# Pinned expert weights, GpSimd stores of the normed rows, and a smaller DMA scratch

## The chip, the cores and the metric

One core of a Trainium2 chip runs the whole program in one launch. The metric is device time in microseconds (us), the median of several runs. One run was also profiled; all rows below are from that execution.

## The reference, cut to what matters

Two layers (DEPTH = 2) of a model of width 1024 over 512 latent tokens and, in the first layer, 256 context tokens. In each layer an attention mix (neighbourhood attention, a gated recurrence, differential attention) is projected by `w_out` and added to `x`; then every token goes to two of 32 experts.

```python
for l in range(2):
    ...                                                    # mix: y_na, y_rg, y_diff
    xl = xl + ga1 * (concat([y_na, y_rg, y_diff]) @ w_out[l])
    hl2 = rmsnorm(xl, g_ffn[l]) * (1 + sc2) + sh2          # "normed rows"
    # two-level router: 1 group of 4, then 2 of its 8 experts
    expert_id, weight = route(hl2)
    # each expert: (silu(x @ w1) * (x @ w3)) @ w2, D = 1024, F = 512
    xl = xl + ga2 * moe(hl2, expert_id, weight)            # layer 0: also the context rows
return rmsnorm(xl, g_final)
```

The kernel loads the weights of all 32 experts in each layer, 32 x 6 tiles of 1 MB: 384 tiles, 402.7 MB of the 544.74 MB that the profile shows read from HBM.

## The kernel before, in words

The kernel is written against a tile framework: code asks for tiles from pools, and a scheduler puts the instructions of each engine in a fixed order. A new tile of a full pool waits until the last reader of the tile that it replaces is done. Every engine runs its own instructions, and its own DMA issues, strictly in order.

Weights. A tile "w" is 128 x 2048 f32, 1 MB. An expert takes six: w1, w3, w2 in two halves each (`eparts`, L1015). The tiles come round robin from the list `wcycle` (L1008): pools `wta` (NWA tiles), `wt2` (NW2 - NWA), `wt` (6, shared with other loads of the stages before) and `wt3` (4); W0 says where in the list the six of `wt` stand. The ring has 6 + 6 + 4 = 16 tiles in layer 0 and 8 + 6 + 4 = 18 in layer 1. All loads go through SyncE's queue (SP), except the first SPIN of a layer, which ScalarE (ACT) issues (L1024).

Pinned experts. The last three experts, 29 to 31 (NPIN = 3), run first, whatever the router says, so that their 18 tiles can be loaded before it has spoken ("pins"). The generator `ping` issues one pin at each call: NWA of them inside the attention stage (L1149), some in the loop over token tiles until PINT are out (L1391), then all but HELD (L1410), and the last HELD only behind `idn` (L1503), the last vector of the routing (L1505). The other 29 experts are sorted by their number of tokens on the chip; their loads need the expert's number (`sid`, L1818).

Loop over token tiles (L1378 on; six in layer 0, four in layer 1). `wmm` is TensorE's projection (L1101); `upd` (L1345) adds it to X on VectorE (L1347), squares it on ACT (L1348) and makes the factor r on GpSimd (L1350, L1351). `normed` (L1354) makes hp = X * r * a2 on VectorE (L1357), adds s2 on VectorE for tiles 1 and 3 (HVV) and on GpSimd for the others (L1358), and stores hp to the DRAM tensor h2d (L1359). `turn_x` transposes X (L1367) and `logits` (L1374) gives the router's values, which L1396 scales by r.

Routing (L1325 to L1503) is a chain of small VectorE instructions with a few matmuls; it ends in idx_t, sid and idn. `weights` (L1780 to L1806) makes the experts' weights for the output, not for the order.

Experts. For each one GpSimd gathers its rows from h2d (`xg`, L1826), TensorE transposes them (L1628), multiplies by w1 and w3 (L1638 for 32 rows, L1642 and L1643 for 64, L1648 for 128), ACT copies the product (`hs`, L1658), TensorE transposes again (L1667, L1672) and multiplies by w2 (L1695, L1700, L1701, L1706); VectorE scales the result (L1562, L1564) and GpSimd scatters it to the DRAM tensor yd (L1517). In layer 0 alone each expert also has its scale made ahead by ACT in a tile "yl" (L1553); there are three such tiles, and one is free again when its scatter has landed.

Of the kernel before, what the change touches and what calls it, by code (L numbers as in the profile page):

```python
# [56 lines left out]
RGR = (1.0, 0.85)  # L57
FLG = (1, 1)
WST = (0, 0)
HELD = (4, 3)  # L60
DMO = ("gsXw", "gsXw")
FLL = (3, 1)
LTS = ("aaatmghsscccbbbbcccccMccocHccc", "")
# [24 lines left out]
UE = ("SV", "SV")  # L88
OSV = ((0, 1), (0, 1))
OHV = ((0, 1, 2, 3, 4, 5), (0, 1, 2, 3, 4, 5))  # L90
SPIN = (2, 0)
PINT = (6, 8)
FEX = (0, 0)
DOR = ("asctwfv", "asctwfv")
CHD = ("TV", "TV")
# [7 lines left out]
AHEAD = 1  # L103
CXN = ((2, 0, 0), (0, 0, 2))
XNB = (6, 2)
NW2 = (6, 8)
NWA = (0, 2)
NWS = (9, 9)
W0 = (4, 12)
LAM = (1, 1)  # L110
DIAG = (1, 1)
SCT = (1, 1)
# [138 lines left out]
def program(tc, a, out, dbg=None):  # L251
    nc = tc.nc
# [22 lines left out]
    V, S, G, T = [Chained(e_) for e_ in (nc.vector, nc.scalar, nc.gpsimd, nc.tensor)]  # L275
    Y = nc.sync
# [9 lines left out]
    h2d = [dr.tile([NT, D], F32, name=f"h2d{l}") for l in range(2)]  # L286
# [165 lines left out]
    for l in range(2):  # L452
# [551 lines left out]
        sid = xp_.tile([1, 33], I32, name="sid")  # L1004
        nw2 = NW2[l] - NWA[l]
        wta = P.open(f"wta{l}")
        wcount, held = [0], [None]
        wcycle = [(lambda: wta, NWA[l])] * NWA[l] + [(lambda: wt2, nw2)] * nw2 + [(lambda: wt3, 4)] * 4  # L1008
        wcycle[W0[l]:W0[l]] = [(wt, 6)] * 6

# [4 lines left out]
        def eparts(e, eng=Y, tail=False):  # L1015
            for nm in ("w1", "w3", "w2"):
# [3 lines left out]
                for h in range(2):  # L1020
                    pl, nb = wcycle[wcount[0] % len(wcycle)]
                    w = wtile(pl() if callable(pl) else pl, nb)
                    wcount[0] += 1
                    held[0] = (Y if wcount[0] > SPIN[l] else eng).dma_start(w.rearrange("p (k f) -> p k f", k=2 * n if cut else n),  # L1024
                                                               src[:, :, 512 * h:512 * h + 512] if cut else src[:, n * h:n * h + n, :])
# [91 lines left out]
        def wparts():  # L1117
            todo = [(hf, t, k0) for hf in range(2) for t in range(nt) for k0 in KO]
            ahead = [ysplit(*z_[1:]) for z_ in todo[:YA[l]]]
            for n_, (hf, t, k0) in enumerate(todo):  # L1120
# [28 lines left out]
                if n_ == NWS[l]:  # L1149
                    for _ in range(NWA[l]):  # L1150
                        next(ping)
# [202 lines left out]
        def normed(t, hp, r1):  # L1354
            a2, s2 = vs[t // 4]
            hv = hp.rearrange("t (k p) -> t p k", p=128)
            V.scalar_tensor_tensor(hv, kp(X[:, t, :]), r1, kp(a2), op0=ALU.mult, op1=ALU.mult)  # L1357
            (V if t in HVV[l] else G).tensor_tensor(hv, hv, kp(s2), op=ALU.add)  # L1358
            Y.dma_start(h2d[l][128 * t:128 * t + 128, :], hp)  # L1359

        def turn_x(t):
            xT2 = op.tile([128, 8, 128], F32, name="xT2", bufs=1)
# [15 lines left out]
        for t in range(nt + 1):  # L1378
            if t < nt:
                k67 = (7,) if t in p6 else (6, 7)  # L1380
                p_ = p6[t] if t in p6 else pss()
                wmm(p_[:, 0:512], t, 0, k67)
            if t > 0:
                xT2 = turn_x(t - 1)
            if t < nt:
                wmm(p_[:, 512:1024], t, 1, k67)
            if t > 0:
                pg = logits(t - 1, xT2)
            if t < nt:
                hps[t] = upd(t, p_)  # L1390
                for _ in range(8 // nt + 1):  # L1391
                    if wcount[0] < PINT[l]:
                        next(ping)
            if t > 0:
                hp, r1 = hps.pop(t - 1)
                V.scalar_tensor_tensor(lg[:, t - 1, :], pg[:, 0:36], r1, crow[(t - 1) // 4], op0=ALU.mult, op1=ALU.add)  # L1396
                normed(t - 1, hp, r1)
            if t == nt - 2:
                top2(0, nt - 2)
# [9 lines left out]

        for _ in range(6 * NPIN - wcount[0] - HELD[l]):  # L1410
            next(ping)
# [710 lines left out]
        for k_ in SEQ[l]:  # L2122
# [4 lines left out]
            else:  # L2127
                combine(*k_)
                if k_[1]:
                    n_, t = k_[0], order[k_[0]]  # L2130
# [32 lines left out]
```

## Time and profile before

| | |
|---|---|
| median of 3 runs | 2043.89 us (2037.6 to 2045.23) |
| profiled execution | 2047.19 us, its span 2045.6 us |
| TensorE busy | 1692.9 us, 83% of the span |
| VectorE, ScalarE, GpSimd busy | 901.0, 575.3, 407.1 us |
| DMA | 579.20 MB, mean 283 GB/s |
| SyncE's queue | 553.35 MB, 71.5% of 16 engines' span |
| GpSimd's queue | 20.87 MB, 2.9% |
| granted TensorE clock, mean | 0.909 of full speed |

In time the program is: layer 0's stages up to about 541 us, its experts to about 1062, a tail to 1111; layer 1's stages to about 1519, its experts to about 1984, and the final sum and norm. Shares over the whole span mix these; each stretch is to be read by itself.

### The profile page before, as it was taken

To read this page: it belongs to the slowest core of one execution; us is meant where nothing else is said; L and a number is where in the kernel's file an instruction comes from. 1 tells how busy PE (TensorE), PEld (TensorE's weight loads), DVE (VectorE), ACT (ScalarE), POOL (GpSimd) and SP (SyncE) were. 2 spreads that over 40 slices of the span, in tenths; PEclk is the share of its full clock that TensorE was granted. 3 is DMA by queue.
4 is the path that set the end of the run, shared out by engine and by line. 5 is a ranking of instruction groups with operands and counts; after the bars stand their busy time and mean duration, and the time that the engine had idled before them with its cause. 6 is when DMAs were issued, how large, how long until landed. Compare 5 with 4: busy or idle time off the path is not lost. (4 is left out here: it accounts for less than half of the span.)

```text
span 2045.6 us, 24880 instructions
## 1 busy us (share of the span) xinstructions
PE 1692.9 (83%) x9306; PEld 975.2 (48%) x9306; DVE 901.0 (44%) x1506; ACT 575.3 (28%) x1033; POOL 407.1 (20%) x394
## 2 busy tenths in 40 slices
PE   4998998899697888889895987887959988879773
PEld 3766666676333333333333977566733333333221
DVE  3876443785622212212227698548662122121225
ACT  3563343662111101111113475346411010010011
POOL 1344000443311011001003145104321110010001
PEclk8999999898698998999896989898969989999886
DMA  8537967606799989989986113346469999999994
GB/s 299 203 131 285 322 225 185 165 37 252 275 409 348 407 344 368 417 325 410 401 342 261 58 51 103 125 111 207 188 228 400 404 414 409 410 413 416 416 392 167
DMA packets 153709, 579.20 MB, mean 283 GB/s; under 512 B 18734, under 2 KB 54958, under 8 KB 114672
## 3 DMA queue, kind: packets, MB, share of 16 engines
q1 hardware_dynamic: 142240, 553.35, 71.5%
q0 software_dynamic: 9328, 20.87, 2.9%
q10 hardware_dynamic: 2016, 3.34, 0.5%
q8 instruction: 75, 1.23, 0.2%
q14 instruction: 50, 0.41, 0.1%
HBM read 544.74 MB, written 42.05 MB: 287 GB/s over the span
## 5 line engine op out<-in xcount | busy, mean ns | idle before, releaser
L491 PE MATMUL mm<-hh,w 128*128 128x256 f32 (+1 forms) x960 | 191.5, 343 | 6.6 <-ACT w L434 4.7
L1643 PE MATMUL pss<-w,xT 128*64 128x512 f32 x368 | 170.7, 611 | 7.3 <-DMA w<-in_w_dram 7.3
L1642 PE MATMUL pss<-w,xT 128*64 128x512 f32 x368 | 175.3, 619 | 0.0
L1638 PE MATMUL pss<-w,xT 128*32 128x512 f32 x880 | 140.4, 686 | 37.2 <-DMA w<-in_w_dram 37.2
L491 PEld LDWEIGHTS mm<-hh,w 128*128 128x128 f32 x960 | 150.1, 193 | 37.7 <-issue 9.8
L1826 POOL DMA_INDIRECT xg<-h2d,idx_t x64 | 61.4, 959 | 515.7 <-PE mm L1628 476.8
L1648 PE MATMUL pss<-w,xT 128*128 128x512 f32 x352 | 156.0, 597 | 0.0
L1658 ACT COPY hs<-pss 128x512 f32<-128x512 f32 x53 | 30.9, 582 | 375.6 <-PE pss L1638 221.9
L1517 POOL DMA_INDIRECT yd<-yl,slots x47 | 44.3, 942 | 383.1 <-DVE yl L1562 204.3
L1700 PE MATMUL pss<-w,hT 128*64 128x512 f32 x184 | 102.0, 698 | 9.2 <-DVE hT L1678 8.9
L1648 PEld LDWEIGHTS pss<-w,xT 128*128 128x128 f32 x352 | 65.3, 190 | 89.1 <-issue 83.3
L1678 DVE TENSOR_TENSOR hT<-hT,mm 128x128 f32<-128x128 f32 (+1 forms) x53 | 18.3, 345 | 196.0 <-ACT hT L1677 195.9
L1701 PE MATMUL pss<-w,hT 128*64 128x512 f32 x184 | 102.0, 698 | 0.0
L1558 DVE SCALAR_TENSOR_TENSOR yl<-g,wsl,yl 64x1024 f32<-64x1024 f32 (+2 forms) x32 | 40.8, 1276 | 129.9 <-ACT yl L1553 129.6
L1638 PEld LDWEIGHTS pss<-w,xT 128*32 128x32 f32 x880 | 32.0, 122 | 137.7 <-issue 74.5
L1553 ACT ACTIVATE yl<-g,wsl 64x1024 f32<-64x1024 f32 (+2 forms) x32 | 36.6, 1147 | 211.2 <-DMA yd<-yl,slots 178.6
L1706 PE MATMUL pss<-w,hT 128*128 128x512 f32 x176 | 91.0, 664 | 3.1 <-issue 3.1
L491 PE MATMUL mm<-hl,w 128*128 128x256 f32 (+1 forms) x480 | 93.2, 336 | 0.1
L1562 DVE TENSOR_TENSOR yl<-pss,yl 64x512 f32<-64x512 f32 (+1 forms) x44 | 29.6, 687 | 138.7 <-PE pss L1701 76.0
L351 DVE COPY xT<-mm 128x512 f32<-128x512 f32 (+1 forms) x64 | 36.2, 566 | 101.2 <-PE mm L1628 100.5
L491 PEld LDWEIGHTS mm<-hl,w 128*128 128x128 f32 x480 | 75.4, 190 | 11.1 <-issue 0.8
L1643 PEld LDWEIGHTS pss<-w,xT 128*64 128x64 f32 x368 | 48.8, 140 | 60.3 <-issue 48.2
(377 smaller groups left out, 3263.4 us busy)
## 6 DMA issues: line engine op xcount, KB each, us to landing
w<-in_w_dram SPq DMA_DIRECT2D x382, 1024.0 KB
w<-in_w_ada_dram SPq DMA_DIRECT2D x48, 1024.0 KB
w<-in_w_in_dram SPq DMA_DIRECT2D x20, 1024.0 KB
yd<-bm SPq DMA_DIRECT2D x20, 512.0 KB
w<-yd SPq DMA_DIRECT2D x10, 1024.0 KB
ks<-st SPq DMA_DIRECT2D x16, 384.0 KB
w<-in_w_out_dram SPq DMA_DIRECT2D x5, 1024.0 KB
h2d<-hp SPq DMA_DIRECT2D x10, 512.0 KB
```

Of the source, the lines that this page charges most:

```text
L491: i_ = T.matmul(o, x_(k), y_(k), start=(n == 0), stop=(n == 23))
L1517: G.indirect_dma_start(out=yd[l][0:2 * nrow, :], out_offset=bass.IndirectOffsetOnAxis(ap=idxt, axis=0), in_=rows, in_offset=None, bounds_c ...
L1553: S.activation(self.u[r], g2[r, 1], AF.Copy, scale=b_)
L1558: (V if eng[1] == "V" else G).scalar_tensor_tensor(self.u[r], g2[r, 0], a_, self.u[r], op0=ALU.mult, op1=ALU.add)
L1638: T.matmul(ph[32 * g:32 * g + 32, 0:512], xT[:, k + g // 2, 0:32], w(k + g // 2), start=(k == 0), stop=(k == 6))
L1642: T.matmul(ph[0:64, 0:512], xT[:, k, 0:64], w1(k), start=(k == 0), stop=(k == 7))
L1643: T.matmul(ph[64:128, 0:512], xT[:, k, 0:64], w3(k), start=(k == 0), stop=(k == 7))
L1648: T.matmul(ph[:, o:o + 512], xT[:, k, :], w(k), start=(k == 0), stop=(k == 7))
L1700: T.matmul(py[0:64, :], hT[:, k, 0:64], w2(k, 0), start=(k == 0), stop=(k == 3))
L1701: T.matmul(py[64:128, :], hT[:, k, 0:64], w2(k, 1), start=(k == 0), stop=(k == 3))
L1706: T.matmul(self.p[:, 512 * hf:512 * hf + 512], hT[:, k, :], w2(k, hf), start=(k == 0), stop=(k == 3))
L1826: G.indirect_dma_start(out=o[0:n_, :], out_offset=None, in_=h2d[l][0:nrow, :], in_offset=bass.IndirectOffsetOnAxis(ap=idxt, axis=0), bound ...
```

## The change

Three things. `normed` issues its store on GpSimd's queue rather than SyncE's. The program reserves 4096 bytes per partition for the descriptors of GpSimd's DMAs; the call before named no size. Seven tables change: a ring of 7 + 6 + 4 = 17 weight tiles in layer 0 and 9 + 6 + 4 = 19 in layer 1, other places of the pools in the ring, one more pin in the attention stage, no pin on ACT's queue, up to 14 pins in the loop, and 1 and 0 pins held behind the routing instead of 4 and 3.

```diff
-HELD = (4, 3)
+HELD = (1, 0)
...
-SPIN = (2, 0)
-PINT = (6, 8)
+SPIN = (0, 0)
+PINT = (14, 14)
...
-NW2 = (6, 8)
-NWA = (0, 2)
+NW2 = (7, 9)
+NWA = (1, 3)
...
-W0 = (4, 12)
+W0 = (7, 9)
...
-            Y.dma_start(h2d[l][128 * t:128 * t + 128, :], hp)
+            G.dma_start(h2d[l][128 * t:128 * t + 128, :], hp)
...
-    nc = bacc.Bacc("TRN2", target_bir_lowering=False, num_devices=1)
+    nc = bacc.Bacc("TRN2", target_bir_lowering=False, num_devices=1, dynamic_dma_scratch_size=4096)
```

The scheduler's order changes with it. SyncE's queue in layer 1, from the loop over token tiles to the first load that needs the routing (sid), before (-) and now (+):

```order
-L1024 DMA w<-in_w_dram 128x2048 x7
+L1024 DMA w<-in_w_dram 128x2048 x4
 L1024 DMA w<-in_w_dram 128x2x1024 x2
 L1024 DMA w<-in_w_dram 128x2048 x2
-L1359 DMA h2d_61<-hp 128x1024 x4
-L1024 DMA w<-in_w_dram 128x2048 x2
 L1024 DMA w<-in_w_dram 128x2x1024 x2
-L1413 DMA g_10724<-ada_58 128x1024
-L1024 DMA w<-in_w_dram 128x2048
+L1024 DMA w<-in_w_dram 128x2048 x6
 L1024 DMA w<-in_w_dram 128x2x1024 x2
+L1413 DMA g_10726<-ada_58 128x1024
 L1818 TENSOR_LOAD sid
```

The four stores are gone from this queue, and all 18 pins stand ahead of the routing's number.

GpSimd's queue in layer 0, at the first token tiles (r is the factor of a tile, hp its normed row), now:

```order
L1350 TENSOR_SCALAR r_4408<-ss 128x1
L1351 TENSOR_TENSOR r_4408<-r_4408,mhalf 128x1
L1358 TENSOR_TENSOR hp<-hp,w 128x128x8
L1359 DMA h2d_60<-hp 128x1024
L1350 TENSOR_SCALAR r_4445<-ss 128x1
L1351 TENSOR_TENSOR r_4445<-r_4445,mhalf 128x1
L1359 DMA h2d_60<-hp 128x1024
L1350 TENSOR_SCALAR r_4486<-ss 128x1
```

The factor of each tile now stands behind the store of the tile before; without the L1359 rows this is the order before.

VectorE's queue in layer 0, at the same tiles, before:

```order
L1347 TENSOR_TENSOR X<-X,pss 128x1024 x2
L1396 SCALAR_TENSOR_TENSOR lg<-acc,r_4406,crow_2987 128x36
L1357 SCALAR_TENSOR_TENSOR hp<-X,r_4443,w 128x128x8
L1358 TENSOR_TENSOR hp<-hp,w 128x128x8
L1396 SCALAR_TENSOR_TENSOR lg<-acc,r_4443,crow_2987 128x36
L1357 SCALAR_TENSOR_TENSOR hp<-X,r_4484,w 128x128x8
```

and now:

```order
L1347 TENSOR_TENSOR X<-X,pss 128x1024
L1396 SCALAR_TENSOR_TENSOR lg<-acc,r_4408,crow_2987 128x36
L1357 SCALAR_TENSOR_TENSOR hp<-X,r_4445,w 128x128x8
L1358 TENSOR_TENSOR hp<-hp,w 128x128x8
L1347 TENSOR_TENSOR X<-X,pss 128x1024
L1396 SCALAR_TENSOR_TENSOR lg<-acc,r_4445,crow_2987 128x36
L1357 SCALAR_TENSOR_TENSOR hp<-X,r_4486,w 128x128x8
```

The sum of token tile 2 (the second of the two L1347) has moved behind the normed row of tile 1. In the routing of layer 0, behind the last one-hot tile (ohb), VectorE now has:

```order
L1335 TENSOR_TENSOR ohb<-oh 128x128
L1436 TENSOR_SCALAR yl<-oh,pidx 128x12x32
L1481 TENSOR_SCALAR t_4798<-cs_83 128x6
L1782 SCALAR_TENSOR_TENSOR t_4389<-m_4388,gs 128x6
L1784 RECIPROCAL wgt<-t_4389 128x6
L1785 TENSOR_TENSOR wgt<-wgt,m_4388 128x6
L1789 CAST w3p<-wgt 128x12
L1442 TENSOR_TENSOR yl<-oh,mm 128x384
```

Before, four more instructions of L1789 and L1791 stood ahead of L1442; they now stand between later rows of the chain. In layer 1 VectorE's order in these two places is as before.

## Rows read from the trace of the kernel before

**Rows 1.** Busy time by stretch: PE, PEld, DVE, ACT, POOL, PEclk, DMA share, GB/s.
```profile
553.00:1062.00 509.00, 442.04 (x1881) 174.81 (x1884) 119.04 (x163) 68.39 (x98) 51.62 (x54) 0.93 0.96 376
1534.00:1984.00 450.00, 379.19 (x2000) 149.13 (x2002) 95.71 (x160) 38.59 (x78) 46.08 (x49) 0.93 1.01 409
```

**Rows 2.** Waits, 545 to 1062 us: us in total, times, longest (PE, PEld, ACT).
```profile
PE mm L1672 <- ACT hs L1658: 44.5, 12, 7.7
...
PEld pss L1643 <- DMA w<-in_w_dram: 1.8, 3, 0.8
...
ACT yl L1553 <- DMA yd<-yl,slots: 178.6, 15, 22.2
```

**Rows 3.** Timeline of one such wait: start, us, what, idle before and its releaser.
```profile
585.04 1.15 ACT L1553 ACTIVATE yl<-g,wsl 128x1024 f32<-128x1024 f32 x1 [9.36 <-DMA yd<-yl,slots]
...
586.72 1.11 PE L1672 MATMUL mm<-cst,hs 128*128 128x128 f32 x4 [4.64 <-ACT hs L1658]
```

**Rows 4.** Waits of PE, 1519 to 1984 us, the longest.
```profile
PE pss L1638 <- DMA w<-in_w_dram: 32.2, 13, 4.5
```

**Rows 5.** Waits of SyncE's queue, 541 to 553 us.
```profile
SPq L1024 <- DVE idn L1503: 12.8, 1, 12.8
SPq L1024 <- PE pss L1642: 8.5, 1, 8.5
```

**Rows 6.** Timeline of SyncE's issues: last early pins, first loads behind a TensorE release.
```profile
525.85 2.50 SPq L1024 DMA_DIRECT2D w<-in_w_dram  x4
...
1527.72 0.36 SPq L1024 DMA_DIRECT2D w<-in_w_dram  x1
```

**Rows 7.** Busy time by stretch: the first and last of layer 0's three long DMA gaps.
```profile
757.00:763.00 6.00, 6.00 (x15) 2.06 (x13) 0.00 (x0) 0.00 (x0) 0.00 (x0) 1.00 0.12 23
...
1025.00:1032.00 7.00, 7.00 (x16) 2.47 (x14) 0.00 (x0) 0.00 (x0) 0.00 (x0) 0.92 0.14 32
```

**Rows 8.** Timeline of DVE and of ACT's square, layer 0's loop over token tiles.
```profile
491.51 1.22 DVE L1347 TENSOR_TENSOR X<-X,pss 128x1024 f32<-128x1024 f32 x1 [1.28 <-PE pss L1101]
...
494.72 1.07 ACT L1348 ACTIVATE hp<-X 128x1024 f32<-128x1024 f32 x1
...
495.56 1.94 DVE L1358 TENSOR_TENSOR hp<-hp,w 128x1024 f32<-128x1024 f32 x1
...
498.15 2.01 DVE L1357 SCALAR_TENSOR_TENSOR hp<-X,r,w 128x1024 f32<-128x1024 f32 x1 [0.50 <-POOL r L1351]
...
504.06 2.02 DVE L1357 SCALAR_TENSOR_TENSOR hp<-X,r,w 128x1024 f32<-128x1024 f32 x1 [1.83 <-POOL r L1351]
```

**Rows 9.** Timeline of POOL, layer 0's loop, and its first gather.
```profile
489.26 2.88 POOL L1358 TENSOR_TENSOR hp<-hp,w 128x1024 f32<-128x1024 f32 x1 [2.12 <-DVE hp L1357]
492.23 0.19 POOL L1350 TENSOR_SCALAR r<-ss 128x1 f32<-128x1 f32 x1
492.50 0.56 POOL L1351 TENSOR_TENSOR r<-r,mhalf 128x1 f32<-128x1 f32 x1
...
495.96 1.53 POOL L1350 TENSOR_SCALAR r<-ss 128x1 f32<-128x1 f32 x1 [2.90 <-ACT hp L1348]
...
522.56 2.85 POOL L1358 TENSOR_TENSOR hp<-hp,w 128x1024 f32<-128x1024 f32 x1 [2.15 <-issue]
...
540.88 1.24 POOL L1826 DMA_INDIRECT xg<-h2d,idx_t  x1 [5.72 <-DVE slots L1494]
```

**Rows 10.** Timeline of DVE, layer 0's routing behind the last ohb.
```profile
530.07 0.79 DVE L1782 SCALAR_TENSOR_TENSOR t<-m,gs 128x6 f32<-128x6 f32 x1
...
534.39 0.54 DVE L1442 TENSOR_TENSOR yl<-oh,mm 128x384 f32<-128x384 bf16 x1
```

**Rows 11.** Timeline of PE, the first expert's transposes in layer 0.
```profile
544.32 1.08 PE L1628 MATMUL mm<-cst,xg 64*128 64x64 f32 x8 [4.05 <-DMA xg<-h2d,idx_t]
```

**Rows 12.** DMA issues of the whole run: gathers, median us to landing at the end.
```profile
xg<-h2d,idx_t POOLq DMA_INDIRECT x64, 6.5
```

**Rows 13.** Timeline of DVE in layer 1's loop, the normed row of token tile 1.
```profile
1481.18 2.04 DVE L1357 SCALAR_TENSOR_TENSOR hp<-X,r,w 128x1024 f32<-128x1024 f32 x1 [1.58 <-POOL r L1351]
```

## The prediction

> **What bounds the kernel now.** I read the busy time by stretch first, because the mean shares mix stages with different limits. In both layers' experts the DMA looks full: share 0.96 at 376 GB/s in layer 0, and 1.01 at 409 GB/s in layer 1 [rows 1]. By these rates a 1 MB tile (1.049 MB) takes 2.79 and 2.56 us.
>
> The waits tell the two layers apart. In layer 0 TensorE hardly waits for weights, 1.8 us in 3 waits for the largest such group, but 44.5 us in 12 waits for the copy L1658 [rows 2]. That copy is late because ScalarE stands at L1553 before it, waiting for a scatter to land, 178.6 us in 15 waits. One case: ScalarE idles 9.36 us for yd, runs L1553 at 585.04, and TensorE has idled 4.64 us when it goes on at 586.72 [rows 3]. The queue of weights even runs out of free tiles: there are three long stretches like the one at 757, where the DMA engines are busy 0.12 to 0.14 and TensorE works without a gap [rows 7]. So layer 0's experts run at the pace of the chain TensorE, VectorE, scatter, ScalarE; loads are ahead of it. In layer 1 the sign is the other: TensorE's longest wait is for w, 32.2 us in 13 waits [rows 4], with the DMA share at 1.01. There the DMA sets the pace, and whatever starts its stream earlier pays.
>
> Ahead of the experts, the loop over token tiles and the routing are a chain of VectorE, ScalarE and GpSimd. In layer 0 VectorE waits in it for r from GpSimd, 0.50 and 1.83 us [rows 8], so a delay of r there is a delay of all that follows.
>
> **The pins no longer held.** In layer 0 SyncE's queue stands 12.8 us behind idn before the held pins, then 8.5 us for a tile that TensorE has to give back [rows 5]. The first wait goes. But the second stays: the ring is full at that point, and the first load beyond it needs the first release of TensorE, before as after. In layer 1 that load is issued at 1527.72 [rows 6], also behind TensorE. What the change gives is therefore not the 12.8 us but one place in the ring: each load waits for the release that the load before it waited for. That is worth one tile where the DMA sets the pace, 2.56 us in layer 1, and nothing in layer 0, where no load is late (unless the rival below is right). Against it in layer 1: the first load beyond the ring now needs sid, and meets the first gather; up to 0.5 us of one tile's 2.56, by estimate.
>
> **Stores on GpSimd: what one costs there.** The trace of before has no plain DMA on GpSimd. From below: a DMA issue of 4 takes SyncE 2.50 us with its waits [rows 6], so 0.6 us or less. From above: GpSimd's own instruction on a 128x1024 tile takes 2.88 us [rows 9]. Nearest to it is a gather, an indirect DMA, with 1.24 us; a store has no index to read, so I take 1.0 us. SyncE's relief is worth nothing: its stores stood among pins that are due much later.
>
> **Layer 0's loop.** Before, GpSimd's add of tile 0 ends at 489.26 + 2.88 = 492.14, and r of tile 1 follows at 492.23 with 0.19 and 0.56 us [rows 9]. Now the store stands between: 493.1, and r is there at 494.0. VectorE's L1357 of tile 1 then runs 494.1 to 496.1 and its add, 1.94 us, to 498.0. Here the new order counts: the sum of tile 2, which ran at 491.51 for 1.22 us [rows 8], stands behind that add and ends at 499.2. The square on ScalarE (1.07 us and a short read) ends at 500.4; the r pair ends at 501.2. So L1357 of tile 2 begins at 501.2 and not at 498.15, 3.0 us late. Tile 3's sum ends at 503.3 or soon after, as L1357 takes 2.01. GpSimd's add of tile 2 is done at 503.3 + 2.9 = 506.2, its store at 507.2, r at 508.0: L1357 of tile 3 comes at 508.0 in place of 504.06, 4.0 us late [rows 8]. One gain is in this: before, r of tile 2 took 1.53 us in place of 0.19, while VectorE's add ran [rows 9]; now it doesn't meet that add. Tiles 4 and 5 keep their order, and their stores stand in gaps of GpSimd. Term: +4.0, bounds +2.5 (a store of 0.6) and +8 (2.9).
>
> By a rule of the Trainium skill the upper bound would be right. "SBUF — State Buffer", section "SBUF: two separate sides", says that descriptors of a DMA issued by GpSimd are written by GpSimd itself, which is locked out of the port while certain VectorE instructions run, and puts such a DMA at about 620 ns alone and 3100 ns beside them. By its two figures the term would be about +2.5 or +8, by estimate. The trace agrees as far as the lock goes (1.53 for 0.19 us [rows 9]); no row shows it for a store.
>
> **Layer 0's routing.** L1442, which the chain waits for, came at 534.39, and L1782 ahead of it at 530.07, 4.3 us [rows 10]. Four rows between them now stand later; what is left before it (L1436, L1481, L1782 with its 0.79 and three short ones) is some 2.05 us. That is 2.3 us earlier, and the moved rows take back 0.4 between later links: −1.9. The routing then ends at +2.1.
>
> **Layer 0's last pins.** The tile that frees pool room for the last five is read last by GpSimd's add of tile 5, 522.56 + 2.85 = 525.4 [rows 9]; with +4 that is 529.4. So part of the pins still starts behind the stage. Behind that point there are now 5 tiles, two halves of a MB for g2 and a half for the store, 6.5 MB, where 4 tiles stood in the issue of 525.85 [rows 6]. At 2.56 to 2.79 us each the DMA engines are busy until 546 to 548. The first gather, at 540.88 before, fed TensorE at 544.32 after 3.4 us of which 1.24 are its issue [rows 9, 11]; now it goes out at about 543 into full engines, and gathers in such traffic take a median of 6.5 us to land [rows 12]. I take +2 and not the full 3 of difference, since part of the stream has drained by then. Bounds 0 and +3. Layer 0's experts start 2.1 + 2 = 4 us late, at about 548, and end so, with nothing gained on the way.
>
> **Layer 1.** VectorE's order doesn't change. L1357 of tile 1 idles 1.58 us for r [rows 13], so the store ahead of r costs its 1.0 and a little order, +1.1; later stores stand in gaps. With −2.56 for the place in the ring and up to +0.5 for the load behind sid: about −1.2 (bounds −2.6 and +3).
>
> **Sum.** +4.1 − 1.2 = +2.9 on the profiled execution's 2047.19, about 2050. This execution is 3.3 above the median of the three, so 2047 as a median.
>
> **Rivals.**
> *The ring pays in layer 0 too.* If 0.96 of share [rows 1] means that the DMA is the pace there, and TensorE's chain only catches up, one more tile fills each of the three long gaps [rows 7] by 2.56, the first wait for a release (8.5 [rows 5]) by as much, and some shorter gaps by as much as two of these: 6 x 2.56 = −15.4. With +4.1 and −1.2 that is −12.5, about 2031. For it: the share, and that pins no longer stand behind 12.8 us. Against: the waits of TensorE for weights in layer 0 are under a microsecond each [rows 2].
> *Stores locked out by VectorE.* Each of the first stores takes about 3 us in GpSimd's queue, with r of the next tile behind it: +2 more for each of four in layer 0 and 2 to 4 in layer 1, which turns the ring's gain there. Then +4 + 8 − 1.2 + 3 = +14, about 2058. It decides from 2 us a store on. For it: 1.53 us for 0.19 beside VectorE's add. Against: the gather's 1.24 us [rows 9], though VectorE is mostly quiet beside it.
> *The scatter waits fall otherwise.* The 12 waits of 44.5 us in layer 0 [rows 2] depend on when a scatter meets the weight stream. With the start moved by some us and another tile of loads ahead, a quarter of them may come or go: ±10, about 2037 or 2057.
> *It does not do what it says*, pins still wait: for layer 0's last five this is in the forecast already; for layer 1 it would cost the 2.56, about 2050, inside the likeliest range.
>
> **How the numbers follow.** 0.5% is 10 us here, about what a measurement of this kernel can tell from no change. Forecast 0.53 (its own range 2040 to 2053: the bounds above, and half of the scatter's swing); ring in layer 0, 0.19; stores locked out, 0.15; scatter waits, 0.13, evenly to both sides. Faster by over 10 us: 0.19 and 0.05 from the scatter's lower side; slower: 0.15 and 0.05, and 0.02 of the forecast. Range 2030 to 2060, which leaves out half of each of the first two rivals and a little of the rest, about 2 in 10.
>
> **What would show it.** In the trace after: L1357 of layer 0's tiles 2 and 3 some 3 and 4 us later within the loop; stores L1359 of about 1 us on GpSimd (2 to 3 where the lock rules); L1442 about 2 us behind L1782; the last pins of layer 0 issued behind GpSimd's last add, and L1628 some 4 us later; TensorE's waits for weights in layer 0 still small, and the long gaps of the DMA still there though shorter. In layer 1 the stretch between the first gather and the last weights is shorter by one tile. I am wrong if the stretch of layer 0's experts itself shrinks by 5 us or more, if layer 1 gains much more than one tile, or if GpSimd's stores take other than 0.6 to 2.9 us.

## The result, and the profile after

Median 2057.59 us (2046.36 to 2061.27, 17 runs) against 2045.02 us for the kernel before (17 runs). The estimated ratio is 1.0052, 95% interval 1.0034 to 1.0070, about +10.6 us; the two medians by themselves lie 12.6 us apart. The forecast was 2047, +2.9, with a range of 2030 to 2060: the sign and the range held, the size did not, and the likeliest case's own range (2040 to 2053) did not hold the time. That the wide range held is luck: it reached so far up for two rivals, stores locked out by VectorE (2058) and other scatter waits (2057), and neither came about. The profiled execution took 2058.92 us (span 2057.3), 11.7 more than that of before.

To find where, I took from each trace the starts of the same few instructions: L1357 makes the normed row of a token tile, L1628 is the first work of TensorE on an expert's gathered rows. The stretches between them, in us ("again" is a second profile of the changed kernel; the others are the experiments below):

```
stretch                                before  after  again   e2     e3     e4     e6    e10
start to L1357 of tile 0, layer 0       487.2  493.0  490.8  486.9  485.7  484.4  488.7  481.3
L1357 of tile 0 to that of tile 5        33.3   37.5   37.5   34.3   37.5   37.5   33.5   37.5
to the first gather                      20.4   19.6   19.6   22.3   22.0   19.6   20.4   19.8
first gather to the first L1628           3.4    7.0    6.8    3.0    3.6    3.2    3.3    3.1
to L1357 of tile 0, layer 1             930.9  930.3  932.7  930.5  938.5  935.9  931.4  929.3
L1357 of tile 0 to that of tile 3        21.8   22.6   22.6   22.6   22.6   22.6   21.8   22.6
to the first gather                      20.4   22.0   22.9   18.1   20.7   20.8   20.0   19.4
first gather to the first L1628           3.2    6.6    6.0    2.9    6.1    2.9    3.2    3.0
to the last matmul of the experts       491.0  488.7  487.7  491.3  487.7  488.7  488.4  489.6
to the last DMA issue                    25.4   25.4   25.4   25.4   25.4   25.4   25.4   25.4
to the end                                8.5    4.4    4.5    9.3    4.2    4.5    4.4    4.3
```

The second column minus the first, before rounding, gives +5.9, +4.2, −0.8, +3.6, −0.6, +0.8, +1.7, +3.4, −2.3, 0 and −4.2: the 11.7.

VectorE in layer 0's loop, the timeline (start, us, engine, line; in brackets the idle time before and what ended it), beside [rows 8]:

```profile
500.12 2.00 DVE L1357 SCALAR_TENSOR_TENSOR hp<-X,r,w 128x1024 f32<-128x1024 f32 x1 [3.87 <-POOL r L1351]
502.15 1.92 DVE L1358 TENSOR_TENSOR hp<-hp,w 128x1024 f32<-128x1024 f32 x1
503.98 1.22 DVE L1347 TENSOR_TENSOR X<-X,pss 128x1024 f32<-128x1024 f32 x1
```

The idle time for r is 3.87 us here and 3.61 us for tile 3, where it was at most 1.83 for these tiles, and the sum of tile 2 stands at 503.98, behind the add. GpSimd in the same place, beside [rows 9]:

```profile
498.34 0.83 POOL L1359 DMA_DIRECT2D h2d<-hp  x1 [0.31 <-POOL hp L1358]
499.25 0.19 POOL L1350 TENSOR_SCALAR r<-ss 128x1 f32<-128x1 f32 x1
```

A store takes 0.6 to 0.8 us, with some 0.3 of idle time between GpSimd's add and it. The second r pair no longer meets VectorE's add (0.18 in place of 1.53).

SyncE's issues in the attention stage of layer 0, before:

```profile
335.40 2.92 SPq L1048 DMA_DIRECT2D qs<-st  x4
344.09 1.73 SPq L1048 DMA_DIRECT2D ks<-st  x4
345.86 3.09 SPq L1065 DMA_DIRECT2D X<-in_x_dram  x4
```

and now:

```profile
345.79 1.75 SPq L1048 DMA_DIRECT2D qs<-st  x4
...
349.54 7.23 SPq L1065 DMA_DIRECT2D X<-in_x_dram  x4
```

In the kernel before, the loads of qs went out right behind L1069, and only those of ks stood for VectorE's yT (L962), 5.7 us. Now those of qs stand 8.7 us for it, from 337.0 on. The loads of X come behind both, and their four issues take 7.23 us in place of 3.09, with 4.9 us of waiting for qs to land where it was 0.7. This place I had not looked at.

The first transposes of the experts in the two layers, beside [rows 11]:

```profile
557.20 1.08 PE L1628 MATMUL mm<-cst,xg 64*128 64x64 f32 x8 [7.57 <-DMA xg<-h2d,idx_t]
...
1538.78 1.11 PE L1628 MATMUL mm<-cst,xg 64*128 64x64 f32 x8 [7.30 <-DMA xg<-h2d,idx_t]
```

TensorE waits 7.57 us for the gather where it waited 4.05. The DMA's share of time (the last column but one) while the first gather of layer 0, issued at 550.19, is under way, and while that of layer 1, issued at 1532.16, is:

```profile
552.00:555.00 3.00, 0.00 (x0) 0.00 (x0) 0.00 (x0) 0.00 (x0) 1.42 (x2) 0.50 0.94 333
...
1535.00:1538.00 3.00, 0.00 (x0) 0.00 (x0) 0.00 (x0) 0.00 (x0) 0.13 (x1) 0.50 0.77 292
```

In layer 0 the engines are full of pins until past 554 (1.02 from 549 to 552); in layer 1 it is a single tile, issued by SyncE at 1532.61, within half a microsecond of the gather.

In the experts little else has moved. From the first L1628 to the last product with w2, layer 0's take as long as before; the columns are those of [rows 1], the first line is before, the second now:

```profile
544.30:1054.20 509.90, 442.91 (x1850) 175.37 (x1854) 115.90 (x161) 67.31 (x97) 52.56 (x55) 0.93 0.96 373
```

```profile
557.20:1066.40 509.20, 442.92 (x1850) 175.84 (x1854) 115.95 (x161) 67.19 (x97) 52.65 (x55) 0.93 0.94 370
```

TensorE still waits there for ScalarE and hardly for weights (1.0 us in 4 waits for the largest group); in layer 1 it waits for weights, a little less than before, beside [rows 2, 4]:

```profile
PE mm L1672 <- ACT hs L1658: 43.9, 12, 5.9
...
PE pss L1638 <- DMA w<-in_w_dram: 27.6, 13, 4.6
```

### The profile page after: what moved, and what is told of

The parts are those of the page before. It is cut to its first block, busy times and chain, and to the rows that moved or that the text cites. A ratio compares the mean times of both kernels' runs of the same rounds, so it can differ in the third digit from the quotient of the medians.

```text
span 2057.3 us, 24908 instructions
## 1 busy us (share of the span) xinstructions
PE 1700.5 (83%) x9306; PEld 981.7 (48%) x9306; DVE 901.0 (44%) x1506; ACT 574.8 (28%) x1033; POOL 418.2 (20%) x404
## 3 DMA queue, kind: packets, MB, share of 16 engines
q10 hardware_dynamic: 1728, 1.24, 0.3%
## 4 chain that ended last, share of the span: by engine, by line
PE 32%; DMA 26%; issue 21%; DVE 12%; ACT 5%; POOL 3%; SPq 0%; POOLq 0%; ACTq 0%; DVEq 0%
DMA w<-in_w_dram 18%; PE mm L491 10%; DMA yd<-yl,slots 3%; PE acc L267 3%; PE pss L267 2%; PE acc L362 2%; PE pss L1638 1%; PE mm L267 1%; PE pss L1648 1%; DVE tt L775 1%; DMA X<-in_x_dram 1%; PE mm L583 1%; POOL xg L1826 1%; PE mm L874 1%; PE pss L1643 1%
## 5 line engine op out<-in xcount | busy, mean ns | idle before, releaser
L1643 PE MATMUL pss<-w,xT 128*64 128x512 f32 x368 | 174.2, 621 | 7.6 <-DMA w<-in_w_dram 7.6
L1642 PE MATMUL pss<-w,xT 128*64 128x512 f32 x368 | 178.9, 629 | 0.0
L1638 PE MATMUL pss<-w,xT 128*32 128x512 f32 x880 | 133.3, 661 | 33.3 <-DMA w<-in_w_dram 32.5
L1700 PE MATMUL pss<-w,hT 128*64 128x512 f32 x184 | 105.4, 717 | 9.8 <-DVE hT L1678 9.6
L1701 PE MATMUL pss<-w,hT 128*64 128x512 f32 x184 | 103.2, 703 | 0.0
L1678 DVE TENSOR_TENSOR hT<-hT,mm 128x128 f32<-128x128 f32 (+1 forms) x53 | 18.3, 345 | 188.9 <-ACT hT L1677 188.8
```

The source lines that it names most:

```text
L1638: T.matmul(ph[32 * g:32 * g + 32, 0:512], xT[:, k + g // 2, 0:32], w(k + g // 2), start=(k == 0), stop=(k == 6))
L1642: T.matmul(ph[0:64, 0:512], xT[:, k, 0:64], w1(k), start=(k == 0), stop=(k == 7))
L1643: T.matmul(ph[64:128, 0:512], xT[:, k, 0:64], w3(k), start=(k == 0), stop=(k == 7))
L1700: T.matmul(py[0:64, :], hT[:, k, 0:64], w2(k, 0), start=(k == 0), stop=(k == 3))
L1701: T.matmul(py[64:128, :], hT[:, k, 0:64], w2(k, 1), start=(k == 0), stop=(k == 3))
```

## The experiments

Each total is a median with the estimated ratio to the kernel before and its interval; the ratio is not the plain quotient of two medians. The kernel before was measured anew beside e1 to e4, e5 to e8 and e9 to e11, with medians of 2047.06, 2048.88 and 2046.76 us, so totals of different groups compare by their ratios. A few microseconds lie inside their intervals; the stretches of the profile tell the parts apart, and each part is judged by several profiles that share it.

**e1: 4 KB of scratch alone.**

```diff
-    nc = bacc.Bacc("TRN2", target_bir_lowering=False, num_devices=1)
+    nc = bacc.Bacc("TRN2", target_bir_lowering=False, num_devices=1, dynamic_dma_scratch_size=4096)
```

> The kernel before with one edit: 4 KB of DMA scratch; stores, ring and tables as before. Theory (place in SBUF): the smaller scratch moves every tile to another address, so the load of qs at L1048 in layer 0 lands on memory that VectorE's yT (L962) gives back late. L1048 is then issued about 10 us later (345 instead of 335 us), X arrives later, and the loop over token tiles starts 4 to 5 us later; nothing else changes by more than a microsecond or two, so about +5 us in all. Rival (the larger ring or the pin in the attention stage makes that wait): L1048 stays at 335 and the time is that of before.

2049.56 us, 1.0004 (0.9982 to 1.0025). The wait came, with old ring, old tables and old stores. SyncE's queue stood 8.7 us for yT at L1048, and TensorE waited in this stage (waited for: us in total, times, longest):

```profile
PE pss L267 <- DMA X<-in_x_dram: 10.3, 1, 10.3
```

Before, TensorE waited 4.9 us for X here. Against the same matmuls of the kernel before, TensorE's are 0.8 us early at 320 and 3.6 late at 400. So the wait is the scratch's doing, and costs 4.4 us by then. At the end of the program it took 4.3 us from the last DMA issue, where before it took 8.5. The two nearly cancel: the mechanism was right, and the total of +5 was not.

In the profiled execution L1357 of tile 0 even came at 486.71, 0.5 ahead of before. TensorE's granted clock (the last column but two) had risen earlier, ahead of the loop; the first line is before, the second e1:

```profile
470.00:490.00 20.00, 20.00 (x69) 12.76 (x70) 5.50 (x8) 2.56 (x6) 3.78 (x5) 0.66 0.76 290
```

```profile
470.00:490.00 20.00, 17.60 (x91) 10.83 (x92) 8.71 (x10) 3.10 (x7) 8.61 (x8) 0.91 0.93 357
```

Before, it had stood at 0.50 of full speed (1.2 GHz) from 470 to 480 us.

**e2: stores on GpSimd alone.**

```diff
-            Y.dma_start(h2d[l][128 * t:128 * t + 128, :], hp)
+            G.dma_start(h2d[l][128 * t:128 * t + 128, :], hp)
```

> The kernel before with one edit: the normed rows are stored from GpSimd's queue; default scratch, old ring and tables. Here VectorE keeps the sum of token tile 2 ahead of the add of tile 1. Theory (the store costs 0.7 us of GpSimd plus some 0.3 before it, and most of the 4.2 us lost in layer 0's loop came from the moved sum): layer 0's loop is 1 to 2 us longer, layer 1's about 1, about +2 us in all. Rival (the store alone makes the loss): loop +4 us in layer 0, about +5 in all.

2043.26 us, 0.9973 (0.9947 to 1.0000). Loop 34.3 us, +1.0; layer 1's +0.8. So the store costs 1 us a loop as long as the sum of tile 2 isn't moved. But the routing of layer 0 grew to 22.3 us: the same trouble as in e3, next. In layer 1 the routing took 18.1 us, 2.3 less than before; there nothing waited for a store.

**e3: the changed kernel with 8 KB.** The one edit is 8192 in place of 4096.

> The changed kernel with 8 KB of scratch in place of 4; ring, tables and stores as changed. Theory (place in SBUF): L1048 in layer 0 no longer waits for VectorE, is issued near 336 us, and the loop over token tiles starts 4 to 5 us earlier than in the changed kernel; the loss in the loop (4 us) and the late first gather (7 us from issue to the transpose) stay. About 2053 us. Rival (the ring's extra pin makes the wait): no difference from the changed kernel, about 2057.

2049.02 us, 1.0012 (0.9993 to 1.0032). L1048 at 334 us; between 320 and 400 TensorE gained 4.8 us on the changed kernel. The gather in layer 0 was expected at 7 us and took 3.6, for a bad reason: it went out 2.4 us later against the loop, when the pins had nearly landed. VectorE in the routing of e3 and, in layer 1, of the changed kernel:

```profile
537.74 0.17 DVE L1481 TENSOR_SCALAR t<-cs 128x6 f32<-128x6 f32 x1 [4.07 <-DMA h2d<-hp]
```

```profile
1525.18 0.17 DVE L1481 TENSOR_SCALAR t<-cs 128x4 f32<-128x4 f32 x1 [4.75 <-DMA h2d<-hp]
```

L1481 is a tiny instruction that needs nothing of the routing. It waits until the last store has landed, and the routing waits behind it. That its tile lies on memory which a normed row has used is my reading; e10 tests it. In layer 0 of the changed kernel L1481 does not wait. In layer 1 of e3 it does not either, but L1442 does:

```profile
1525.04 0.42 DVE L1442 TENSOR_TENSOR yl<-oh,mm 128x256 f32<-128x256 bf16 x1 [2.53 <-DMA h2d<-hp]
```

**e4: the changed kernel with the held pins of before.**

```diff
-HELD = (1, 0)
+HELD = (4, 3)
```

> The changed kernel with the held pins of before (4 in layer 0, 3 in layer 1 behind the routing); ring of 17 and 19, scratch and stores as changed. Theory (the first gather queues behind weight tiles that are now issued just ahead of it): from issue of the gather to the first transpose L1628 it takes about 3.5 us again in both layers instead of 7 and 7, the experts start 3 to 4 us earlier in each layer, and the ring's gain in layer 1 stays: about 2050 us. Rival (the gather is slow because of the small scratch or of the stores on the same queue): still about 7 us, no gain; and if the pins' early issue was worth something, slower than the changed kernel.

2046.74 us, 1.0002 (0.9980 to 1.0023). The DMA is idle when the gather goes out at 541.61, and the transpose comes 3.2 us after it, at 544.78:

```profile
540.00:543.00 3.00, 0.51 (x5) 0.16 (x4) 2.76 (x25) 0.00 (x0) 1.54 (x3) 0.50 0.00 0
```

Layer 1: 2.9 in place of 6.6 us, and its expert stretch stays at 488.7. So holding pins back costs the ring nothing, and releasing them early bought nothing.

**e5: the kernel before with 8 KB.**

> The kernel before with one edit: 8 KB of DMA scratch. Theory (a smaller scratch shortens GpSimd's DRAIN at the end from 10 us to 4 or 5, which takes about 4 us off the end; at 8 KB the place of qs is harmless): DRAIN 4 to 5 us, from the last DMA issue to the end about 4.3 us in place of 8.5, no wait of L1048 at 343 us, layers as before; about -4 us, some 2042 where before is 2046. Rival (the end varies from run to run, or depends on the ring): 8.5 us at the end as before, no difference.

2041.97 us, 0.9970 (0.9942 to 0.9998). L1048 at 334.67, GpSimd's long DRAIN at the end 3.03 us (4 to 5 expected), 4.3 us from the last issue to the end. The total is as expected, and the layers are as before.

**e6: 8 KB and one more tile in layer 1 alone.**

```diff
-NW2 = (6, 8)
-NWA = (0, 2)
+NW2 = (6, 9)
+NWA = (0, 3)
-W0 = (4, 12)
+W0 = (4, 9)
```

> The kernel before with 8 KB of scratch and one more weight tile in layer 1 alone (ring of 19); stores on SyncE, layer 0's tables and the held pins (4 and 3) as before. Theory (the extra tile is worth 2.6 to 3.3 us in layer 1, where the DMA sets the pace, and costs nothing without the other parts; the end is 4 us shorter): from the first transpose to the last expert matmul in layer 1 about 488 us in place of 491, the first gather about 3 us; -6 to -7 us in all, about 2039 where before is 2046. Rival (the ring's gain is only the later start of the stretch, not a gain of the extra tile): that stretch stays at 491, and the total gains the 4 us of the end alone.

2042.05 us, 0.9972 (0.9950 to 0.9994). The stretch of layer 1 is 488.4 us. All six profiles listed with a ring of 19 have 487.7 to 489.6 there, the two with 18 have 491.0 and 491.3 (not in the table: e7, e9 and e11 with 19 have 489.5, 485.5 and 489.2, e1 and e5 with 18 both 492.7): means of 488.3 and 491.9. That e6 is no faster than e5 in total doesn't speak against it: 3 us lie inside the intervals.

**e7: both repairs, 8 KB and HELD = (4, 3).**

> The changed kernel with 8 KB of scratch and the held pins of before (4 and 3), that is both repairs together; ring 17 and 19, stores on GpSimd. Theory (the waits add up): no wait of L1048 (4.5 us), first gathers of about 3 us in both layers (3.6 and 3.4 us), loop of layer 0 still 37.5 us, about 2 us lost where VectorE's L1481 waits for the last store; about 2043. Rival (what one repair gives the other takes, since both only move the same start of the experts): no better than with one repair, 2047 to 2049.

2041.46 us, 0.9970 (0.9947 to 0.9993). No wait of the loads of qs at L1048, gathers 3.0 us in both layers, loop 37.5, routing of layer 0 21.9. The repairs add up.

**e8: the changed kernel again**, unchanged.

> The changed kernel once more, for a second profile. What comes from its order comes again: L1048 waits for yT and PE for X, layer 0's loop 37.5 us, the first gather about 7 us in both layers, layer 1's expert stretch 488 to 489 us, DRAIN 5 us. What comes from TensorE's granted clock (the stretch at half clock at 480 to 490 us) need not. Rival (the 7 us of the first gathers were one execution's accident): a gather of 3 to 4 us here.

2058.68 us, 1.0059 (1.0034 to 1.0083). Loop, gathers (6.8, 6.0), ring and end came again; L1048 as well, at a price of 5.3 us between 320 and 400. TensorE's clock from 470 to 490 us was 0.66 in both profiles of the changed kernel.

**e9: the changed kernel with the stores back on SyncE.** The edit of e2, undone.

> The changed kernel with the stores back on SyncE's queue (4 KB, ring 17 and 19, held 1 and 0 as changed). VectorE's sum of token tile 2 stays behind the add of tile 1, though no store stands on GpSimd. Theory (the moved sum costs 3.2 of the 4.2 us, the store 1.0): layer 0's loop 36.3 to 36.6 us, between 33.3 and 37.5; SyncE's stores stand behind pins, so the first gather comes later than in the changed kernel or as late. Rival (the sum and the store cost only together): loop 33 to 34 us.

2047.49 us, 1.0009 (0.9985 to 1.0033). Loop 35.4, below the 36.3 to 36.6 that I expected: the moved sum alone costs 2.1 us, the store alone 1.0, both together 4.2. The theory that they add is off by 1.1, the rival (only together) by more. L1048 waited here too, and the gathers took 5.2 and 5.9. Layer 0's routing took 22.7 us, with L1436, L1442 and L1481 late in VectorE's order again: their early place comes with the store on GpSimd (e2 has it), not with the tables.

**e10: e7 with t128 elsewhere.**

```diff
-        t128 = wk_.tile([128, nt], F32, name="t128")
+        t128 = rt.tile([128, nt], F32, name="t128")
```

> The kernel of 8 KB and held pins 4 and 3 (e7) with one edit: the small tile t128 of L1481 comes from another pool, whose memory no normed row has used. Theory (L1481 waits for the landing of the last store, because its tile lies on that row's memory, and the routing stands behind it): from the last L1357 to the first gather in layer 0 some 19.6 us or less in place of 21.9, layer 1 as it was or 1 us shorter; about -2 us against e7, some 2040. Rival (L1442 waits for the same landing anyway): no change in that stretch.

2035.60 us, 0.9944 (0.9923 to 0.9966). L1481 no longer waits, so it was its tile's place. Layer 0's routing took 19.8 us, 2.1 less than in e7; layer 1's 19.4 in place of 19.6. The rival holds in part, for other instructions now stand for the same landing: L1445 in layer 0,

```profile
533.46 2.04 DVE L1445 TENSOR_SCALAR oneh<-iob,pos 128x128 bf16<-128x128 bf16 x12 [1.50 <-DMA h2d<-hp]
```

and L1442 in layer 1, 1.24 us (1.38 in e7). The ratio fell from 0.9970 to 0.9944, some 5 us, with intervals that overlap; what goes beyond the 2 us of the routing I can't place. The clock from 470 to 490 us was 0.92 in this profile and 0.95 in e11's, against 0.73 in e7's; but e1 and e4, with t128 in its old place, had 0.91, so a higher clock there does not need this edit.

**e11: what paid, together**: e10 with layer 0's tables as before, stores on GpSimd, layer 1's ring 19.

> The parts that paid, together: the kernel before with 8 KB of scratch, one more weight tile in layer 1, t128 in the other pool, stores on GpSimd, layer 0's tables as before, held pins 4 and 3. Theory: loop of layer 0 34.3 us (sum of tile 2 not moved), gathers of 3 us, layer 1's expert stretch 488, 4 us less at the end; about 2037 to 2040 us, -7 to -9 against before. Rival (the store's cost in the loops, 1 us each, and the landing of the stores eat what it gives over the kernel with stores on SyncE): no better than e6, 2042.

2037.07 us, 0.9956 (0.9934 to 0.9977). Loop 34.3, routing 18.3, gathers 3.1 and 3.0, layer 1's experts 489.2, 4.6 at the end. e10 and e11 are not told apart by their intervals; both beat the kernel before and the changed one.

## Why the prediction came out as it did

The prediction names three signs of being wrong, and none showed: layer 0's experts got 0.7 us shorter and not 5, layer 1 gained about one tile, and a store took 0.6 to 0.8 us. The loss lay in places that the signs do not watch.

- **What bounds the kernel.** Right. No gain in layer 0's experts from a larger ring (509.9 us before, 509.2 and 509.9 in the two profiles of the changed kernel), and about one tile in layer 1: −2.56 forecast; −2.3 between the first two profiles, −3.6 between the means of all. The five profiles with a ring of 19 whose first transposes are not late (e4, e6, e7, e10, e11) have 489.1 on the mean, −2.8.
- **Store on GpSimd.** 1.0 us taken; 0.6 to 0.8 and 0.3 before it. The rival of stores locked out by VectorE, about 3 us each, fell: no store in layer 0's loop took over 0.84 us. The measured time is nearly that of this rival, 2058, by other causes. The long figure that the Trainium skill gives for such a DMA beside a VectorE copy ("SBUF — State Buffer", section "SBUF: two separate sides") did not show in these rows; the lock itself did, at L1436 below.
- **Layer 0's loop.** +4.0 forecast, +4.2 measured, and tile by tile as forecast: tile 2 came 3.3 us late and tile 3 4.2, against 3.0 and 4.0. e2 and e9 show the split: 2.1 for the order that the tables set, 1.0 for the store, and 1.1 only where both meet.
- **Layer 0's routing.** −1.9 forecast, −0.8 measured in both profiles of the changed kernel. I read the new order as so many short instructions. But L1436 took 2.67 us in place of 0.31: it now runs beside GpSimd's L1433 and MEMSETs, and ends 0.1 us behind the last of them.

```profile
540.18 2.67 DVE L1436 TENSOR_SCALAR yl<-oh,pidx 128x384 bf16<-128x384 bf16 x1
```

```profile
540.90 1.83 POOL L1435 MEMSET xg<- 128x1024 f32 x2
```

In e2, e3, e7, e10 and e11 it had the same neighbours, ended 0.1 us behind L1433 and took 0.89 us; why it also stood for the MEMSETs in the three profiles with stores on GpSimd and 4 KB stays open. A second wait was missing, though not in this layer of the changed kernel: L1481's for the last store, 4.0 to 4.3 us in e2, e3 and e7 (+1.6 for the stretch in e3). In e11, with L1436 at 0.89 and no such wait, the stretch took 18.3 us, −2.1: there the forecast gain came.

- **First gather, layer 0.** +2 forecast with bounds 0 and +3; +3.6 and +3.4. Right in mechanism, too small: I took part of the stream as drained by then, and the engines were full until 554.
- **First gather, layer 1.** This is a step that failed: "up to 0.5 us" for the load behind sid. That load goes out 0.5 us after the gather, and the gather then takes 2.8 to 3.4 us longer, about the length of a whole tile. I priced what the load loses and not what the gather loses.
- **Layer 1 before the gather.** +1.1 for the store ahead of r; 0.8 measured. The 1.7 to 2.5 us in the routing were not in the sum. The prediction has VectorE's order unchanged there, as the section on the change has it; that is wrong. By the traces L1481 ran behind the last ohb before (1512.56, ohb at 1506.85) and stands ahead of it now (1525.18, ohb at 1525.51). The new order by itself is a gain: in e2, which has it too and waits for no store, the routing took 18.1 us, 2.3 less than before. In the changed kernel L1481's wait of 4.75 us made a loss of it; with 8 KB L1442 waits instead, 1.2 to 2.5 us, and the routing takes 19.4 to 20.7 us.
- **The other rival.** The waits for the scatter in layer 0 stayed as they were here (43.9 us in 12 waits, 44.5 before). In other profiles that part did swing: from the first L1628 to the last product with w2 layer 0's experts took 503.7 us in e9, with 36.6 us of these waits and a clock of 0.93, and 516.9 us in e3, with 41.2 us and a clock of 0.91. These swings are in the table's row up to layer 1's loop, so it says little of the edits.
- **The scratch.** The step that failed most, because it had no term at all: the prediction does not name the scratch. It cost 4.4 to 5.3 us at L1048, and gave back 4 at the end of the program. That the cost comes of a new address is the likeliest reading, since it is there with 4 KB and not with 8 KB or the default; no run shows the addresses themselves.

With the measured terms: +4.8 (L1048, of the profiles with that wait) + 4.2 − 0.8 + 3.5 + 0.8 + 2.1 + 3.1 − 3.6 − 4.1 = +10.0, beside +10.6 measured. So close a sum is partly chance: several terms differ by 0.5 to 1 us between profiles. The clock just ahead of the loop differs between executions too, and in e1 it made the way from 470 us to the loop 4.3 us shorter than before; one pair of profiles could not have shown these terms. Why the clock falls there in some executions and not in others stays open.

## What to carry to other kernels

Where a change alters the size of any buffer, look at the waits of the whole program, not at the places that the diff names: a tile that has moved can wait for whoever used its memory before, and a tiny instruction in an in-order queue (L1481) makes a long chain wait for a store that only the gathers at its end need. A load issued early is not free when a small, urgent transfer comes just behind it; hold it back until that transfer is out (e4), if nothing waits for the load.

## What the runs showed that I had not expected

GpSimd's long DRAIN at the end of the program, before and with 8 KB alone (e5); the durations are the shortest, median and longest of three, in ns:

```profile
L2159 POOLq DRAIN  x3: 46/113/10137, 2034.6 to 2045.3; - x3
```

```profile
L2159 POOLq DRAIN  x3: 46/112/3031, 2035.4 to 2041.9; - x3
```

It takes 10.14 us with the default scratch and 10.95 with the stores on GpSimd as well (e2); with 4 KB it is 3.8 with the stores on SyncE and 5.1 with them on GpSimd, with 8 KB 3.0 and 4.4, the same in each of the eleven profiles. It starts some 2.4 us ahead of the last DMA issue, so it sets the end only with the default: 8.5 and 9.3 us from that issue to the end, against 4.2 to 5.5 in the others. Its length is not in proportion to the scratch, and why 4 KB takes longer than 8 I can't say.
